# Prompt attention scores of a hybrid decoder step: six 64-row matmuls per key block in place of four 128-row ones

## The chip, the cores and the metric

One core of a Trainium2 chip runs the whole program. The metric is the device time of one execution in microseconds, as the median of several runs. TensorE does the matmuls (PE in the profile, its weight loads PEld), VectorE (DVE), ScalarE (ACT) and GpSimd (POOL) do the elementwise work, SyncE (SP) starts transfers.

## The reference, cut to what matters

The program is one inference step of a two-layer decoder. Layer 0 has, beside a gated MLP, a differential attention with 8 heads. Each head has two components `c` of 64 channels, and the scores of both are taken for every block of 128 queries against all earlier keys; the rest of the step is not touched by the change.

```python
q = rms_norm(zq.reshape(b, l, H_A, 2, DH_A), q_g) * (DH_A ** -0.5)
k = rms_norm(zk.reshape(b, l, H_A, 2, DH_A), k_g)
s = jnp.einsum('bqhcd,bkhcd->bhcqk', q, k)       # + bias, causal
p = jax.nn.softmax(s, axis=-1)
a = p[:, :, 0] - lam * p[:, :, 1]                # o = a @ v
```

The prompt has 1024 tokens (8 blocks of 128); a ninth unit of each head holds 64 sample tokens, whose scores are computed elsewhere.

## The kernel before, in words

The prompt attention is the first stage, lines 261 to 507. It walks over 72 units (head `h`, block `i`), 9 per head, in a software pipeline: at step `s` it emits `otrans` of unit s-12, `av2` of s-8, `av` of s-6, `scores` of s-5, `qk_trans` of s-2 and the projection `qkv_tile` of s, which is 24 matmuls with 384 columns each (three products of high and low halves, lines 143 to 145). The order in which it emits is a priority only. The tile framework simulates the program while it builds it (`schedule_with_timeline_sim`), and at each moment gives an engine the first instruction in that order whose inputs and buffers are free in the simulation; each engine then runs its list in that fixed order. So instructions of one call can be spread out in an engine's list, and another cost of one instruction can change the list.

All matmuls in question take operands in fp32r, in one pass. To keep the accuracy of fp32, each value is split into a high part and a low part (value minus high part).

`qk_trans` (line 361) turns one block of normalised queries and keys (128 tokens by 128 channels: component 0 in channels 0 to 63, component 1 in 64 to 127) with two transposes on TensorE (L364, L365). Then, for each component in turn, on 64 partitions, it makes the high part of q (L89, called from line 380), the low part of q (L381), a copy of both to the other 64 partitions (L87, called from line 382, on ScalarE), the high part of k (L91, from line 383) and the low part of k into the other 64 partitions (L384). So the 128 rows of a stacked operand hold, for one component, high q twice, or low q twice, against high k over low k.

`scores` (line 387) then has for each block of up to 512 keys and each component two matmuls over 128 rows (L399): high q against (high k, low k), and low q against the same. They add up all four products. The result stands in PSUM under the tag `s`, which has two buffers of two banks each. For i below 4, both components share one buffer, one bank each. For i of 4 and more, each component takes a buffer of its own, so a unit takes both. After the matmuls come, per component, the bias (L405) and the maximum (L407, or one L409 for both), and the exponential (L412, ScalarE), whose end frees the buffer.

Keys stand in `kts[h, j]`, four blocks each; queries in `qs`, two buffers. Unit (h, i) has key blocks j = 0 .. i // 4, with widths 512 for a whole one and 128, 256, 384 or 512 for the last one.

Of the kernel before, what the change touches and what calls it, by code (L numbers as in the profile page):

```python
# [11 lines left out]
F32R = mybir.dt.float32r  # L12
I32 = mybir.dt.int32
AF = mybir.ActivationFunctionType
ALU = mybir.AluOpType
# [9 lines left out]
P = 128  # L25
KT = D // P
H = 8
DH = 64
# [9 lines left out]
PRM = {'ktc': 'a', 'ev': 'p', 'ekm': 'p', 'qem': 'd', 'gm': 2, 'wp': (3, 6), 'at': 'a', 'LQ': 2, 'LS': 5, 'LA': 6, 'L2': 8, 'LO': 12, 'on': 'a', 'oT': 'a', 'qk4': 'p', 'kh': 'd', 'vt': 'a', 'qkc': 'a', 'sq': 'p', 'kg': 'p', 'at0': 'a', 'at1': 'a', 'qh': 'd', 'onm': 'd', 'TS': True, 'p0': 2, 'p1': 2, 'qkb': 3, 'qhb': 2, 'ksb': 3, 'lpq': 2, 'qd': 'a', 'vb': 16, 'atb': 2, 'onb': 4}  # L38
# [24 lines left out]
def rows(i):  # L63
    return P if i < NT - 1 else NS
# [7 lines left out]
def hybrid_step(  # L72
# [8 lines left out]
    pe, act, dve, pool = nc.tensor, nc.scalar, nc.vector, nc.gpsimd  # L81
# [3 lines left out]
    def cpy(e, o, i_, scale=None):  # L85
        if e == 'a':
            act.activation(o, i_, AF.Copy, scale=scale) if scale is not None else act.copy(o, i_)  # L87
        elif scale is not None:
            G[e].tensor_scalar_mul(o, i_, scale)  # L89
        else:  # L90
            G[e].tensor_copy(o, i_)  # L91

    def f32(a):
        return a.bitcast(F32)
# [18 lines left out]
    def const(shape, name, dt=F32):  # L113
        return cp.tile(shape, dt, name=name)
# [68 lines left out]
    if True:  # L183
# [77 lines left out]
        with ExitStack() as p1:  # L261
            pa = p1.enter_context(tc.tile_pool(name="pa", bufs=2))
# [4 lines left out]
            qg = const([P, 1], "qg")  # L267
# [50 lines left out]
            kts, vts = {}, {}  # L318
# [42 lines left out]
            def qk_trans(h, i, qk):  # L361
                r = rows(i)
                tp = ps.tile([P, 512], F32, tag="t", name=f"qkt{h}_{i}", bufs=3)
                pe.transpose(tp[:, 0:r], qk[:r, 0:128], ident[:r, :r])  # L364
                pe.transpose(tp[:, 128:128 + r], qk[:r, 128:256], ident[:r, :r])  # L365
                if i == NT - 1:
                    for c in range(2):
                        q8 = slice(c * DH, (c + 1) * DH)
                        act.activation(qbd[q8, h, :, h // 4, c, :], tp[q8, 0:NS].rearrange("p (b q) -> p b q", b=NB),
                                       AF.Copy, scale=qg[q8])  # L370
                    dve.tensor_copy(ksT[:, h, :], tp[:, 128:128 + NS])
                    return None
                qs = pa.tile([P, 2, 2, P], F32R, tag="qs", name=f"qs{h}_{i}", bufs=PRM["qhb"])
                if i % KW == 0:
                    kts[h, i // KW] = pa.tile([P, 2, KW * P], F32R, tag="ks", name=f"ks{h}_{i}", bufs=PRM["ksb"])
                ks = kts[h, i // KW]
                o = i % KW * P
                for c in range(2):
                    own, oth = slice(c * DH, (c + 1) * DH), slice((1 - c) * DH, (2 - c) * DH)
                    cpy(PRM['qh'], qs[own, c, 0], tp[own, 0:128], qg[own])  # L380
                    dve.scalar_tensor_tensor(qs[own, c, 1], tp[own, 0:128], qg[own], f32(qs[own, c, 0]), ALU.mult, ALU.subtract)  # L381
                    cpy(PRM['qd'], qs[oth, c], f32(qs[own, c]))
                    cpy(PRM['kh'], ks[own, c, o:o + P], tp[own, 128:256])
                    dve.tensor_tensor(ks[oth, c, o:o + P], tp[own, 128:256], f32(ks[own, c, o:o + P]), ALU.subtract)  # L384
                return (qs,)

            def scores(h, i, qs):
                n = (i + 1) * P
                if i < 4:
                    st = ps.tile([P, 2, 512], F32, tag="s", name=f"s{h}_{i}")  # L390
                    sc = [st[:, 0, :], st[:, 1, :]]
                else:
                    sc = [ps.tile([P, 1024], F32, tag="s", name=f"s{h}_{i}_{c}") for c in range(2)]
                for j in range(i // KW + 1):
                    k0 = KW * P * j
                    w = min(KW * P, n - k0)
                    for c in range(2):
                        for l in range(2):
                            pe.matmul(sc[c][:, k0:k0 + w], qs[:, c, l], kts[h, j][:, c, :w], start=(l == 0), stop=(l == 1))  # L399
                nm = pa.tile([P, 2], F32, tag="nm", name=f"nm{h}_{i}")  # L400
                ss = pa.tile([P, 2], F32, tag="ss", name=f"ss{h}_{i}")
                pt = []
                lo = max(0, n - 256)
                for c in range(2):
                    dve.tensor_tensor(sc[c][:, lo:n], sc[c][:, lo:n], tb[:, h, 256 - (n - lo):], ALU.add)  # L405
                    if i >= 4:
                        dve.tensor_reduce(nm[:, c:c + 1], sc[c][:, :n], axis=AX.X, op=ALU.max, negate=True)  # L407
                if i < 4:
                    dve.tensor_reduce(nm, st[:, :, :n], axis=AX.X, op=ALU.max, negate=True)  # L409
                for c in range(2):  # L410
                    pc = pa.tile([P, 1024], F32, tag="p0" if c == 0 else "p1", name=f"p{h}_{i}_{c}", bufs=PRM['p0'] if c == 0 else PRM['p1'])
                    act.activation(pc[:, :n], sc[c][:, :n], AF.Exp, bias=nm[:, c:c + 1], accum_out=ss[:, c:c + 1])  # L412
                    pt.append(pc)
                rr = pa.tile([P, 2], F32, tag="rr", name=f"rr{h}_{i}", bufs=4)
                fac = pa.tile([P, 1], F32, tag="fac", name=f"fac{h}_{i}")
                dve.reciprocal(rr, ss)
                dve.scalar_tensor_tensor(fac, ss[:, 0:1], neglam, rr[:, 1:2], ALU.mult, ALU.mult)
                dve.scalar_tensor_tensor(pt[0][:, :n], pt[1][:, :n], fac, pt[0][:, :n], ALU.mult, ALU.add)  # L418
                return pt[0], rr
# [65 lines left out]
            for s in range(len(units) + max(8, PRM['LO'] + 1)):  # L485
                if s == len(units) - 2:
                    load_gate(0)
                stage(s, PRM['LO'], otr)
                stage(s, PRM['L2'], av2)
                stage(s, PRM['LA'], av)  # L490
                stage(s, PRM['LS'], scores)
                stage(s, PRM['LQ'], qk_trans)
                if 0 <= s - 1 < len(units) and units[s - 1][1] == NT - 1:
                    stage(s, 1, qkv_post)
                if 1 <= s <= NT - 4:
                    xprep(s + 3)
                if s == 1:
                    bias_setup(pa, ps, tb)
                if 20 <= s < 20 + H:
                    bias_sample(tb, s - 20)  # L500
                if s < len(units):
                    h, i = units[s]
                    if i == 3 and h + 1 < H:
                        load_head(h + 1)
                    st_[h, i] = qkv_tile(h, i, Ws[h])
                elif s - len(units) < NPRE:
                    gate_a(*du[s - len(units)], gate_tiles)
# [384 lines left out]
    with ExitStack() as p4:  # L892
# [129 lines left out]
        for n, (c0, cw) in enumerate(CH):  # L1022
            tp = psd.tile([P, 512], F32, tag="x", name=f"rbp{n}", bufs=4)
            for q in range(3):
                i = n * 3 + q
# [390 lines left out]
        i = NT - 1  # L1416
# [79 lines left out]
```

## Time and profile before

| | us |
|---|---|
| median of 3 runs | 1801.37 |
| lowest and highest run | 1799.54, 1802.87 |
| span of the profiled execution | 1806.1 |
| PE busy in the span | 1747.1 |
| DVE busy in the span | 1012.4 |
| ACT busy in the span | 755.4 |

The profile is of one execution; its span is 4.7 us above the median of the runs. PE busy counts modelled ends of pipelined matmuls that overlap, so it is no measure of the work in the array; from the start of one matmul to the start of the next is the better one. "PEclk" is the clock that TensorE was granted, in parts of full speed.

### The profile page before, as it was taken

To read this page: it belongs to the slowest core of one execution; us is meant where nothing else is said; L and a number is where in the kernel's file an instruction comes from. 1 tells how busy PE (TensorE), PEld (TensorE's weight loads), DVE (VectorE), ACT (ScalarE), POOL (GpSimd) and SP (SyncE) were. 2 spreads that over 40 slices of the span, in tenths; PEclk is the share of its full clock that TensorE was granted. 3 is DMA by queue.
4 is the path that set the end of the run, shared out by engine and by line. 5 is a ranking of instruction groups with operands and counts; after the bars stand their busy time and mean duration, and the time that the engine had idled before them with its cause. 6 is when DMAs were issued, how large, how long until landed. Compare 5 with 4: busy or idle time off the path is not lost.

```text
span 1806.1 us, 31855 instructions
## 1 busy us (share of the span) xinstructions
PE 1747.1 (97%) x11429; PEld 1629.0 (90%) x11429; DVE 1012.4 (56%) x2223; ACT 755.4 (42%) x1934; POOL 609.3 (34%) x893
## 2 busy tenths in 40 slices
PE   7999999999999899999899999999999999998999
PEld 6798999999999888889899999999999999996777
DVE  5898888988983233223832342444354455667442
ACT  4566656666664222223222232333343334345241
POOL 4555646655653221112721200044111232235230
PEclk8999999999999999999999999999999999999999
DMA  7102202211213766746221262432334244438741
GB/s 211 52 23 73 68 20 67 67 43 43 66 59 104 243 202 232 236 165 213 59 79 54 92 199 74 129 97 82 94 116 152 80 126 123 130 111 260 240 130 71
DMA packets 223302, 211.62 MB, mean 117 GB/s; under 512 B 22286, under 2 KB 201143, under 8 KB 223143
## 3 DMA queue, kind: packets, MB, share of 16 engines
q1 hardware_dynamic: 203510, 194.35, 34.7%
q10 hardware_dynamic: 19632, 15.21, 2.8%
q8 instruction: 91, 1.49, 0.4%
q14 instruction: 69, 0.56, 0.1%
HBM read 151.35 MB, written 56.24 MB: 115 GB/s over the span
## 4 chain that ended last, share of the span: by engine, by line
PE 62%; DVE 16%; DMA 9%; ACT 4%; POOL 4%; issue 4%; SPq 0%; ACTq 0%; POOLq 0%; DVEq 0%
PE o L1373 5%; PE yo L143 3%; PE yo L145 3%; PE yo L144 3%; PE vg L143 3%; PE vg L144 3%; PE vg L145 3%; DMA oT_d<-oTr 2%; DVE p L418 2%; PE zv L143 1%; PE zv L144 1%; PE zv L145 1%; PE o L434 1%; PE s L399 1%; PE qkv L143 1%
## 5 line engine op out<-in xcount | busy, mean ns | idle before, releaser
L412 ACT ACTIVATE p<-s,nm 128x256 f32<-128x256 f32 (+7 forms) x128 | 95.0, 747 | 38.3 <-DVE nm L409 22.3
L399 PE MATMUL s<-ks,qs 128*128 128x512 f32 (+3 forms) x384 | 96.5, 364 | 2.8 <-DVE ks L384 1.4
L87 ACT CAST qs<-qs 64x256 fp32r<-64x256 f32 x128 | 51.7, 404 | 76.8 <-DVE qs L381 74.2
L1120 POOL TENSOR_TENSOR e<-e,k 128x256 f32<-128x256 f32 (+1 forms) x50 | 42.4, 853 | 117.1 <-ACT e L1117 100.8
L338 POOL TENSOR_TENSOR sq<-qk 128x256 f32<-128x256 f32 (+1 forms) x72 | 46.9, 652 | 95.0 <-ACT qk L87 94.2
L434 PE MATMUL o<-v,at 128*128 128x128 f32 x576 | 76.8, 279 | 1.6 <-ACT at L87 1.6
L399 PEld LDWEIGHTS s<-ks,qs 128*128 128x128 f32 x384 | 64.9, 190 | 12.6 <-ACT p L412 2.8
L434 PEld LDWEIGHTS o<-v,at 128*128 128x128 f32 x576 | 71.4, 193 | 4.2 <-ACT at L87 2.6
L131 POOL TENSOR_TENSOR s<-s,mhalf 128x4 f32<-128x4 f32 (+1 forms) x72 | 73.3, 1018 | 5.3
L837 DVE TENSOR_TENSOR yp<-yp,yo 128x384 f32<-128x384 f32 (+1 forms) x48 | 25.3, 530 | 74.5 <-ACT yp L836 41.7
L407 DVE TENSOR_REDUCE nm<-s 128x1 f32<-128x640 f32 (+3 forms) x64 | 65.2, 1019 | 1.2
L747 POOL TENSOR_TENSOR u<-u,th 128x384 f32<-128x384 f32 (+1 forms) x24 | 28.7, 1194 | 99.9 <-DVE th L746 99.4
L405 DVE TENSOR_TENSOR s<-s,tb 128x256 f32<-128x256 f32 (+1 forms) x128 | 52.8, 412 | 8.9 <-PE s L399 5.6
L418 DVE SCALAR_TENSOR_TENSOR p<-p,fac,p 128x128 f32<-128x128 f32 (+3 forms) x64 | 55.1, 861 | 1.7
L1373 PE MATMUL o<-w1h,oh 128*128 128x512 f32 x128 | 53.0, 414 | 2.5 <-ACT oh L1350 2.5
L87 ACT COPY at<-atp 128x512 f32<-128x512 f32 (+2 forms) x96 | 44.5, 481 | 20.0 <-PE atp L427 19.8
L746 DVE SCALAR_TENSOR_TENSOR th<-th,gb 128x384 f32<-128x384 f32 (+1 forms) x24 | 12.6, 524 | 69.0 <-ACT th L745 69.0
L1373 PE MATMUL o<-w1l,oh 128*128 128x512 f32 x128 | 50.8, 397 | 0.0
L1373 PE MATMUL o<-w1h,ol 128*128 128x512 f32 x128 | 50.3, 407 | 0.0
L427 PE MATMUL atp<-cf,p 128*128 128x128 f32 x288 | 46.8, 275 | 1.9 <-DVE p L418 1.8
L343 POOL TENSOR_TENSOR qk<-qk,s 128x256 f32<-128x256 f32 (+1 forms) x72 | 46.6, 647 | 4.7
L381 DVE SCALAR_TENSOR_TENSOR qs<-qkt,qg,qs 64x128 fp32r<-64x128 f32 x128 | 44.5, 348 | 3.6
(825 smaller groups left out, 6340.4 us busy)
## 6 DMA issues: line engine op xcount, KB each, us to landing
kp<-in_cache_k SPq DMA_DIRECT2D x32, 512.0 KB
vp<-in_cache_v SPq DMA_DIRECT2D x32, 512.0 KB
or<-oT_d SPq DMA_DIRECT2D x16, 384.0 KB
vb_d<-zs SPq DMA_DIRECT2D x36, 128.0 KB
oT_d<-ob SPq DMA_DIRECT2D x8, 544.0 KB
gt<-g_d SPq DMA_DIRECT2D x34, 128.0 KB
xt<-in_x_prompt SPq DMA_DIRECT2D x8, 512.0 KB
out<-v ACTq DMA_DIRECT2D x64, 64.0 KB
```

The costliest lines, as they stand in the source:

```text
L87: act.activation(o, i_, AF.Copy, scale=scale) if scale is not None else act.copy(o, i_)
L131: pool.tensor_tensor(dst, dst, mhalf[:dst.shape[0], :n], ALU.pow)
L143: pe.matmul(out, lh, rh, start=(s == 0), stop=False)
L144: pe.matmul(out, lh, rl, start=False, stop=False)
L145: pe.matmul(out, ll, rh, start=False, stop=(s == n - 1))
L399: pe.matmul(sc[c][:, k0:k0 + w], qs[:, c, l], kts[h, j][:, c, :w], start=(l == 0), stop=(l == 1))
L405: dve.tensor_tensor(sc[c][:, lo:n], sc[c][:, lo:n], tb[:, h, 256 - (n - lo):], ALU.add)
L407: dve.tensor_reduce(nm[:, c:c + 1], sc[c][:, :n], axis=AX.X, op=ALU.max, negate=True)
L412: act.activation(pc[:, :n], sc[c][:, :n], AF.Exp, bias=nm[:, c:c + 1], accum_out=ss[:, c:c + 1])
L418: dve.scalar_tensor_tensor(pt[0][:, :n], pt[1][:, :n], fac, pt[0][:, :n], ALU.mult, ALU.add)
L434: pe.matmul(op[:, :P], at[:, j * P:(j + 1) * P], vts[h, j], start=(j == 0), stop=(j == i))
L1373: pe.matmul(it.mp[:r], lh[:, k, :r], rh[k][:, cs], start=(k == 0 and a == 0), stop=(k == KT - 1 and a == 2))
```

## The change

Component 0 stays in partitions 0 to 63 and component 1 in 64 to 127. `qk_trans` makes the high and low parts of q and k over all 128 partitions at once, for both components: four VectorE instructions per unit in place of eight, and no copy on ScalarE. `scores` has three products per key block and component (high by high, high by low, low by high; low by low is dropped), each a matmul over the 64 rows of its component, and runs the two components in turn for each product. The two components of one product use different rows of the array and different PSUM banks.

```diff
-                qs = pa.tile([P, 2, 2, P], F32R, tag="qs", name=f"qs{h}_{i}", bufs=PRM["qhb"])
+                qs = pa.tile([P, 2, P], F32R, tag="qs", name=f"qs{h}_{i}", bufs=PRM["qhb"])
...
-                for c in range(2):
-                    own, oth = slice(c * DH, (c + 1) * DH), slice((1 - c) * DH, (2 - c) * DH)
-                    cpy(PRM['qh'], qs[own, c, 0], tp[own, 0:128], qg[own])
-                    dve.scalar_tensor_tensor(qs[own, c, 1], tp[own, 0:128], qg[own], f32(qs[own, c, 0]), ALU.mult, ALU.subtract)
-                    cpy(PRM['qd'], qs[oth, c], f32(qs[own, c]))
-                    cpy(PRM['kh'], ks[own, c, o:o + P], tp[own, 128:256])
-                    dve.tensor_tensor(ks[oth, c, o:o + P], tp[own, 128:256], f32(ks[own, c, o:o + P]), ALU.subtract)
+                cpy(PRM['qh'], qs[:, 0], tp[:, 0:128], qg)
+                dve.scalar_tensor_tensor(qs[:, 1], tp[:, 0:128], qg, f32(qs[:, 0]), ALU.mult, ALU.subtract)
+                cpy(PRM['kh'], ks[:, 0, o:o + P], tp[:, 128:256])
+                dve.tensor_tensor(ks[:, 1, o:o + P], tp[:, 128:256], f32(ks[:, 0, o:o + P]), ALU.subtract)
...
-                    for c in range(2):
-                        for l in range(2):
-                            pe.matmul(sc[c][:, k0:k0 + w], qs[:, c, l], kts[h, j][:, c, :w], start=(l == 0), stop=(l == 1))
+                    for l, (ql, kl) in enumerate(((0, 0), (0, 1), (1, 0))):
+                        for c in range(2):
+                            cr = slice(c * DH, (c + 1) * DH)
+                            pe.matmul(sc[c][:, k0:k0 + w], qs[cr, ql], kts[h, j][cr, kl, :w], start=(l == 0), stop=(l == 2))
```

## Rows read from the trace of the kernel before

**Rows 1.** The page: busy us, share of the span, instructions of each engine.
```profile
PE 1747.1 (97%) x11429; PEld 1629.0 (90%) x11429; DVE 1012.4 (56%) x2223; ACT 755.4 (42%) x1934; POOL 609.3 (34%) x893
```

**Rows 2.** Busy time by stretch, columns PE, PEld, DVE, ACT, POOL, PEclk, DMA, GB/s.
```profile
45.00:553.00 508.00, 495.30 (x3089) 464.86 (x3088) 447.88 (x1121) 326.26 (x958) 291.35 (x509) 0.99 0.18 54
...
553.00:1806.00 1253.00, 1217.84 (x8174) 1134.61 (x8172) 541.20 (x1063) 409.10 (x934) 297.83 (x349) 0.99 0.45 139
```

**Rows 3.** Waits, 45 to 553 us: who waited for whom, us, times, longest.
```profile
PEld s L399 <- ACT p L412: 2.8, 7, 0.6
...
PEld s L399 <- ACT qs L87: 2.4, 5, 0.5
...
PE s L399 <- DVE ks L384: 1.4, 4, 0.4
```

**Rows 4.** Instructions by form, 45 to 553 us: count | busy us, mean ns | idle before.
```profile
L399 PE MATMUL s<-ks,qs 128*128 128x512 f32 x192 | 62.3, 424 | 1.2 <-ACT p L412 1.0
L87 ACT CAST qs<-qs 64x256 fp32r<-64x256 f32 x128 | 51.7, 404 | 76.8 <-DVE qs L381 74.2
L381 DVE SCALAR_TENSOR_TENSOR qs<-qkt,qg,qs 64x128 fp32r<-64x128 f32 x128 | 44.5, 348 | 3.6
L89 DVE TENSOR_SCALAR qs<-qkt,qg 64x128 fp32r<-64x128 f32 x128 | 44.3, 346 | 3.3 <-PE qkt L365 1.3
L384 DVE TENSOR_TENSOR ks<-qkt,ks 64x128 fp32r<-64x128 f32 x128 | 36.9, 288 | 4.1
L91 DVE CAST ks<-qkt 64x128 fp32r<-64x128 f32 x128 | 36.0, 281 | 0.0
...
L89 DVE TENSOR_SCALAR on<-on,ms 128x128 f32<-128x128 f32 x60 | 23.9, 398 | 6.9 <-POOL ms L131 5.8
```

**Rows 5.** Chain of waits, 100 to 200 us: start, us; L399 with widths 512, 256, 384, 128.
```profile
109.33 1.11 PE o L434 x10
110.45 0.93 PE s L399 x4
...
118.93 0.24 PE s L399 x2
...
126.38 0.35 PE s L399 x2
...
178.67 0.18 PE s L399 x2
```

**Rows 6.** PE in order of time, 399 to 405 us: start, us.
```profile
399.96 0.96 PE L399 MATMUL s<-ks,qs 128*128 128x512 f32 x4 [0.15 <-ACT p L412]
...
403.72 0.94 PE L399 MATMUL s<-ks,qs 128*128 128x512 f32 x4
```

**Rows 7.** ACT in order of time, 399 to 402 us.
```profile
399.03 0.78 ACT L412 ACTIVATE p<-s,nm 128x640 f32<-128x640 f32 x1
...
400.54 0.81 ACT L412 ACTIVATE p<-s,nm 128x640 f32<-128x640 f32 x1
```

**Rows 8.** PE, then PEld, in order of time, 67 to 70 us.
```profile
67.35 0.52 PE L399 MATMUL s<-ks,qs 128*128 128x384 f32 x2
67.81 0.46 PE L309 MATMUL xtp<-cf,xn 64*128 64x64 f32 x4
68.19 0.62 PE L399 MATMUL s<-ks,qs 128*128 128x384 f32 x2
68.75 0.46 PE L309 MATMUL xtp<-cf,xn 64*128 64x64 f32 x4
...
67.81 0.32 PEld L309 LDWEIGHTS xtp<-cf,xn 64*128 64x128 f32 x4 [0.26 <-DVE xl L138]
...
69.13 0.19 PEld L143 LDWEIGHTS qkv<-wq0h,xh 128*128 128x128 f32 x1
69.24 0.19 PEld L144 LDWEIGHTS qkv<-wq0l,xh 128*128 128x128 f32 x1
```

**Rows 9.** PE in order of time, 617 to 621 us: the sample scores' 32-column tiles.
```profile
617.78 1.92 PE L550 MATMUL ssc<-kT,qbd 128*32 128x512 f32 x16
```

## The prediction

> **What bounds the kernel now.** I read the page first, then the busy times by stretch, then the waits of the attention stage, and last TensorE's instructions in order of time. PE is busy for 97% of the span [rows 1], and in the stage that the change touches (45 to 553 us) for 495 of 508 us, at a granted clock of 0.99; DVE is at 448, ACT at 326 [rows 2]. So TensorE's own list of instructions sets the stage, with 12.7 us in which it isn't busy at all. The waits agree: what TensorE waits for from the operands and buffers of the scores are single microseconds in total, 2.8, 2.4 and 1.4 [rows 3]. DVE is close behind, but a faster DVE can give back no more than those 12.7 us, as long as TensorE's list isn't shorter. The 1253 us after the stage have PE at 97% too and none of the changed code [rows 2], so what the stage gains or loses, the end gains or loses.
>
> **Elementwise work.** Per unit, the change takes away four DVE instructions and two ACT copies, and makes four DVE instructions twice as tall. The price of an instruction on 64 partitions is 346 ns (L89), 348 (L381), 281 (L91) and 288 (L384), each 128 times [rows 4]. An L89 of the same 128 columns over 128 partitions took 398 ns [rows 4], on another operand, so I take height as nearly free: 64 units at 1.26 us less, 81 us of DVE (70 if all cost 398), and 51.7 us of ACT. Both engines have idle time beside TensorE, so of that only what TensorE waits for counts: at least 0, at most 12.7 us [rows 2]. I take 8, near the 6.6 us of the three waits on what the change makes shorter [rows 3].
>
> **The score matmuls, if they ran as written.** In the chain of waits, runs without a stall give the time of one matmul from start to start: 0.93 us for four of 512 columns, so 0.23; 0.24 for two of 256, so 0.12; 0.35 for two of 384, 0.175; 0.18 for two of 128, 0.09 [rows 5]. With four products, a head has for i below 4 (one width each) 4 x (0.09 + 0.12 + 0.175 + 0.23) = 2.46 us, and for i from 4 to 7 the same plus four whole blocks, 2.46 + 4 x 0.93 = 6.18 us. Eight heads: 69 us (the counts agree: 192 matmuls of 512 columns [rows 4]). If the two components of a product run side by side, three pairs stand in place of four matmuls, a quarter less: -17.3 us. If they run one after the other, six stand in place of four: +34.6 us. Nothing in this kernel runs 64-row tiles side by side, but 32-column tiles do: 16 records of 512 columns took 1.92 us [rows 9], where ten records of the same type with 128 columns take 1.11, so 0.44 for one of 512 and 7.1 for 16 [rows 5]. That is nearly four at a time, so I take it that two row tiles overlap too. The Trainium skill (TensorE: Matmul & The Clock Gate, Part 3) says the same of row tiles, starts about 4 ns apart, but gives a measured 3.07x for four; an estimate by that share (0.77 of ideal) would leave almost nothing of the gain of a pair. No run here shows it.
>
> **Which of them are side by side.** This decides the sum. For i of 4 and more, each component has its own PSUM buffer, and a unit needs both; a buffer comes free when the exponential of the unit before has read it. Those ends lie apart: the exponentials of i = 4 begin at 399.03 and 400.54 [rows 7], and the scores of i = 5 stand in TensorE's list at 399.96 (the wait is on L412) for component 0 and at 403.72 for component 1, with projections between [rows 6]. In all 32 such units the two components are separate runs, 1 to 7 us apart, as in these rows. In the changed text, high by high of component 0 is followed by that of component 1, whose buffer isn't free yet; the planner passes over it, as it does now, and takes the next two products of component 0. So these units get three products on one half of the array, alone, and later three on the other half: 6.18 becomes 9.27, +3.1 a head, +24.7 us. For i below 4 both components share one buffer. They are apart now too, but there the second component's operands are made after the first's; in the change both come at once, so I take them as pairs: -0.62 a head, -4.9 us. The other end is that two weight loads don't overlap: a load took 0.11 us before the next could start [rows 8], six make 0.66, which for the narrow blocks is more than now (0.36, 0.48) and gives +1.7 us in place of -4.9.
>
> **Going in and out of 64-row tiles.** This trace has 64-row matmuls among 128-row ones. From 67.35 to 68.19 us, two matmuls of 384 columns (0.35) and four 64-row transposes (loads 0.06 apart, 0.24) take 0.84: 0.25 too much. The two matmuls of 384 behind them take 0.56 up to the next transposes, where the first two took 0.46: another 0.10 [rows 8]. So a trip costs 0.35 us, and the first fp32r load inside it isn't hidden either (0.11 against the transposes' 0.06): 0.40. Every run of scores becomes a trip. Units with i of 4 and more have two runs each, 64 in all, the others one, 32: 96 x 0.40 = +38.4 us. Its lower end is 0.20, where a trip begins in a stall that is there anyway, as at 399.96.
>
> **Sum.** +24.7 - 4.9 + 38.4 - 8 = +50 us on the profiled span of 1806.1, so 1856; the median of the runs is 4.7 below the span: 1851. I say 1850. With the lower ends (trips at 0.20, the full 12.7 back) it is 1801.4 + 24.7 - 4.9 + 19.2 - 12.7 = 1828, with the upper ends (nothing back, loads in turn) 1801.4 + 24.7 + 1.7 + 38.4 = 1866. The stage's transposes, projections and transfers are neither more nor fewer; the copy's queue, ACT, is only shorter.
>
> **Rivals.**
> (1) All components are paired, because the planner's list, with half the DVE work and no copy, no longer finds the second buffer late. For it speaks that the list comes from a simulation that I don't see, and that the planner gives the paired products the better place in the order once both buffers are free; against it, that a buffer's release hangs on L412 and the maximum before it, which don't change. Then there are 64 trips: -17.3 + 25.6 - 12.7 (TensorE's list hardly grows, so DVE's relief reaches it in full) = -4.4, 1797. It decides below (17.3 + 12.7) / 0.40 = 75 trips: with fewer the kernel is faster. I give it 18 in 100, just over half of that on the faster side.
> (2) No pair overlaps, or all components are split, for i below 4 too: 34.6 + 128 x 0.40 - 8 = +78, 1879. For it, that nearly all of them are split now; against it, the shared buffer. 12 in 100.
> (3) The trips are mostly hidden (0.10 each) with the same split: 24.7 - 4.9 + 9.6 - 8 = +21, 1823. Against it stands [rows 8], where nothing hid them. 8 in 100.
> (4) In a run on one half of the array each weight load waits for the matmul before it: 64 runs of three or six matmuls, 384 in all, 0.11 us each, +42 on my sum, 1893. The Trainium skill (the same page, Part 3, what overlaps) would have it so, loads overlapping only where the row group differs. The trace speaks against it: the four 64-row transposes, all on the same rows, have loads 0.06 apart that take 0.14 each [rows 8]. 2 in 100.
> That the change doesn't do what it says is no rival of its own: rival 2 holds it.
>
> **How the numbers follow.** My forecast has 60 in 100, the rivals 18, 12, 8 and 2. Of the forecast and rivals 2 to 4 all is slower, 82 in 100. Rival 1 gives 10 to faster by over 0.2% and 8 to within 0.2%, which is about 3.6 us and about what a measurement of this kernel can tell from no change. The range from 1800 to 1880 holds the forecast with its ends (1828 to 1866), rivals 2 and 3, and the upper half of rival 1; left out are the lower half of rival 1, rival 4 and a tail of the second.
>
> **What would show it.** In the changed profile, TensorE's list for i of 4 and more has runs of one component, six matmuls in a row at 0.23 or less from start to start, and component 1 some us later; for i below 4, L399's successor has pairs that start within hundredths of a microsecond. About 0.4 us more than the matmuls' own time lies around each run, as in [rows 8]. DVE's busy time in the stage falls by about 80 us and ACT's by 52, and the stage ends about 50 us later. I am wrong if the runs hold both components for i of 4 and more, if the trips cost much less than 0.4, or if TensorE waits for something else by then.

## The result and the profile after

The change makes the kernel slower: 1825.35 us against 1800.53 (medians of four runs each), a ratio of 1.0128, 95% interval 1.0106 to 1.015. So it costs 23 us by the ratio (19 to 27) and 25 by the medians, half of the 50 that were forecast, and on the forecast's side of no change. The profiled execution after has a span of 1827.4 us, before 1806.1: 21.3 more.

The page of the changed kernel, engines and the costliest group of the scores (in this kernel the score matmuls stand on L397):

```profile
PE 1784.9 (98%) x11621; PEld 1640.0 (90%) x11621; DVE 924.6 (51%) x1967; ACT 700.6 (38%) x1806; POOL 615.8 (34%) x893
...
L397 PE MATMUL s<-ks,qs 64*128 64x512 f32 (+3 forms) x576 | 107.0, 369 | 0.0
```

The busy times of the attention stage, same columns as [rows 2]:

```profile
45.00:553.00 508.00, 507.45 (x3143) 453.64 (x3142) 343.45 (x837) 257.77 (x795) 285.90 (x495) 1.00 0.17 50
```

The elementwise part did what was forecast: in the same 508 us DVE has 343 us of work where it had 448, ACT 258 where it had 326 (not all of the stage: it ends later now). PE is busy for 507.45 of 508 us; the 12.7 us in which it was not are gone. The elementwise instructions by form, 45 to 575 us, answer to [rows 4]:

```profile
L379 DVE SCALAR_TENSOR_TENSOR qs<-qkt,qg,qs 128x128 fp32r<-128x128 f32 x64 | 22.1, 345 | 0.9
...
L89 DVE TENSOR_SCALAR qs<-qkt,qg 128x128 fp32r<-128x128 f32 x64 | 22.0, 344 | 14.7 <-PE qkt L365 13.7 <-PE s L397 0.4
...
L381 DVE TENSOR_TENSOR ks<-qkt,ks 128x128 fp32r<-128x128 f32 x64 | 18.1, 283 | 0.5
...
L91 DVE CAST ks<-qkt 128x128 fp32r<-128x128 f32 x64 | 17.8, 279 | 0.0
```

128 partitions cost what 64 did (344 ns against 346 for L89), with half as many instructions: about 80 us of DVE gone, and the copies with them.

Now TensorE in order of time, where head 2 turns to i = 4 (projections left out), and then i = 7 of the same head:

```profile
203.99 1.02 PE L397 MATMUL s<-ks,qs 64*128 64x512 f32 x4
204.93 0.33 PE L364 MATMUL qkt<-cf,qk 128*128 128x128 f32 x1
205.10 0.27 PE L365 MATMUL qkt<-cf,qk 128*128 128x128 f32 x1
205.30 0.43 PE L397 MATMUL s<-ks,qs 64*128 64x128 f32 x2
205.66 0.44 PE L143 MATMUL qkv<-wq2h,xh 128*128 128x384 f32 x1
205.94 0.34 PE L144 MATMUL qkv<-wq2l,xh 128*128 128x384 f32 x1
...
210.04 0.39 PE L432 MATMUL o<-v,at 128*128 128x128 f32 x2
210.36 1.24 PE L397 MATMUL s<-ks,qs 64*128 64x512 f32 x6
211.53 0.55 PE L425 MATMUL atp<-cf,p 128*128 128x128 f32 x3
```

```profile
233.26 1.65 PE L397 MATMUL s<-ks,qs 64*128 64x512 f32 x12
234.84 0.44 PE L143 MATMUL qkv<-wq3h,xh 128*128 128x384 f32 x1
235.12 0.34 PE L144 MATMUL qkv<-wq3l,xh 128*128 128x384 f32 x1
```

In the first, one component's six matmuls (three of 512 columns, three of 128) stand at 203.99 and 205.30, and the other's six at 210.36: apart by 6 us, as forecast, and alone on their half of the array. Besides, two transposes got between the first six, so they make two trips. In the second, all twelve matmuls of i = 7 stand in one run, and it takes 1.58 us up to the next start. Twelve one after the other would take 12 x 0.23 = 2.76. Less about 0.19 for the run's first weight load and for getting out, it is 0.23 for each pair: two row tiles do run side by side, at the price of one. (The two of a pair start 1 to 10 ns apart in this run.) The trip can be read here too: 0.44 stands for a projection of 384 columns that is 0.34 otherwise, and 0.28 lies between its start and the next, where it is 0.17.

I then took the stage apart for every kernel in the same way: from the first score matmul to the last transposed output (54.8 to 579.1 us before, 54.7 to 601.0 after), less the time that each matmul has when nothing disturbs it. These are 0.174 us for 384 columns, 0.148 for 320, 0.11 for one fp32 record of 128, and for scores 0.23, 0.175, 0.12 and 0.09 by width, a pair that starts together (less than 15 ns apart) counted once. What is left is trips and waits; trips are counted in TensorE's list (from a 128-row to a 64-row matmul, all lines) and taken at 0.37 us, of which 0.09 is ahead of the run, 0.10 its first load, 0.09 behind it, and 0.06 to 0.11 the first load of what follows. The last column is a rest, good to a few us. Read gap by gap instead, with no fixed price, the gaps at 64-row matmuls and right behind them have 44 us beyond the undisturbed times after (0.34 a trip), and all other gaps have 3 us after and about 30 before. The profile's own list of waits agrees in kind: what it names for PE and its loads from 45 to 560 us, without what it puts down to "issue", adds up to 39 us before and 10 after.

| kernel | stage | scores' own time | trips | trips x 0.37 | waits (rest) |
|---|---|---|---|---|---|
| before | 524.3 | 68.5 | 11 | 4 | 32 |
| after | 546.3 | 78.4 | 127 | 47 | 1 |
| difference | +22.0 | +9.9 | +116 | +43 | -31 |

All other matmuls are 420 us in both. Behind the stage nothing changed: 1227.0 us are left before, 1226.4 after.

So the result is +10 for the matmuls, +43 for the trips and -31 for waits that are gone, where the forecast had +20, +38 and -8. The question for the experiments was what took the waits away: the lighter elementwise work, or TensorE's longer list, behind which waits disappear. A third possibility goes with both: the planner builds each kernel's list anew, and another order can have other waits.

### The profile page after: what moved, and what is told of

The parts are those of the page before. It is cut to its first block, busy times and chain, and to the rows that moved or that the text cites. A ratio compares the mean times of both kernels' runs of the same rounds, so it can differ in the third digit from the quotient of the medians.

```text
span 1827.4 us, 31816 instructions
## 1 busy us (share of the span) xinstructions
PE 1784.9 (98%) x11621; PEld 1640.0 (90%) x11621; DVE 924.6 (51%) x1967; ACT 700.6 (38%) x1806; POOL 615.8 (34%) x893
## 4 chain that ended last, share of the span: by engine, by line
PE 82%; DMA 7%; DVE 4%; issue 2%; POOL 2%; ACT 2%; SPq 0%; ACTq 0%; POOLq 0%; DVEq 0%
PE s L397 5%; PE qkv L143 5%; PE o L1371 5%; PE qkv L144 5%; PE qkv L145 5%; PE o L432 4%; PE yo L143 3%; PE yo L145 3%; PE yo L144 3%; PE vg L143 3%; PE vg L144 3%; PE vg L145 3%; PE atp L425 2%; PE zv L143 2%; PE zv L144 2%
## 5 line engine op out<-in xcount | busy, mean ns | idle before, releaser
L397 PE MATMUL s<-ks,qs 64*128 64x512 f32 (+3 forms) x576 | 107.0, 369 | 0.0
L397 PEld LDWEIGHTS s<-ks,qs 64*128 64x128 f32 x576 | 70.4, 184 | 24.5 <-issue 10.8
L87 ACT COPY qk<-qkv 128x256 f32<-128x256 f32 x64 | 23.7, 370 | 150.9 <-issue 116.4
L340 DVE TENSOR_REDUCE s<-sq 128x4 f32<-128x256 f32 (+1 forms) x72 | 29.9, 415 | 75.5 <-POOL sq L338 75.4
```

Source lines behind the costliest of these rows:

```text
L397: pe.matmul(sc[c][:, k0:k0 + w], qs[cr, ql], kts[h, j][cr, kl, :w], start=(l == 0), stop=(l == 2))
```

## The experiments

Each kernel's expectations were written before it ran; ratios are to the kernel before, run on the same chip.

**The elementwise part alone.** Scores in `e1_prep_alone`, with the change's `qk_trans`:

```diff
-                    for l, (ql, kl) in enumerate(((0, 0), (0, 1), (1, 0))):
-                        for c in range(2):
-                            cr = slice(c * DH, (c + 1) * DH)
-                            pe.matmul(sc[c][:, k0:k0 + w], qs[cr, ql], kts[h, j][cr, kl, :w], start=(l == 0), stop=(l == 2))
+                    for c in range(2):
+                        for l in range(2):
+                            pe.matmul(sc[c][:, k0:k0 + w], qs[:, l], kts[h, j][:, c, :w], start=(l == 0), stop=(l == 1))
```

> The elementwise part of the change alone: four VectorE instructions over 128 partitions and no copies, with the four 128-row matmuls of before on these operands (so the scores mix both components; the output is not the reference's). No 64-row tiles, the same matmul time as before. Theory: the lighter elementwise work gives TensorE back about 27 us, so 1774. Rival, as the forecast had it: it gives back about 8, so 1792.

1790.7 us, ratio 0.9966 (0.9948 to 0.9984). That is 6 to 8 us faster (3 to 9 by the interval), the forecast's 8, and not the 27 of the theory that I had formed from the trace of after. With TensorE's list nearly as long as before (17 trips in place of 11), waits fall from 32 to 21 us, and new ones show up, which the waits from 45 to 560 us name:

```profile
PEld o L431 <- ACT at L87: 10.8, 14, 2.4
...
PE o L431 <- ACT at L87: 6.4, 11, 2.0
```

TensorE now waits for the transposed weights `at` that ACT copies, a wait of 2.6 us in the kernel before (the loads' part):

```profile
PEld o L434 <- ACT at L87: 2.6, 5, 0.5
```

So the lighter work alone doesn't explain the 31 us.

**Six matmuls over all 128 rows.** No 64-row tiles, no pairs: the longest list that the scores can have.

```diff
-                            cr = slice(c * DH, (c + 1) * DH)
-                            pe.matmul(sc[c][:, k0:k0 + w], qs[cr, ql], kts[h, j][cr, kl, :w], start=(l == 0), stop=(l == 2))
+                            pe.matmul(sc[c][:, k0:k0 + w], qs[:, ql], kts[h, j][:, kl, :w], start=(l == 0), stop=(l == 2))
```

> The changed kernel with its six matmuls per key block over all 128 rows instead of 64 (the scores mix both components; the output is not the reference's): no trips into 64-row tiles and no overlap of the two components. Theory: +34.6 us for six matmuls in place of four and -27 for the lighter elementwise work, 1808, so faster than the change. Rival: the trips are cheap and the elementwise work gave little, then this is 1800.5 + 34.6 - 8 = 1827, no faster than the change.

1812.5 us, ratio 1.0076 (1.0053 to 1.0098): between the theory's 1808 and the rival's 1827, nearer to the theory (though the 27 in it isn't what the elementwise part gives alone), and faster than the change, although nothing runs side by side in it. Against the run before, the list is longer by 34 us and the time by 21.8; waits fall from 21 to 7. Over a third of the added work isn't in the time: as much of the waits is gone.

**The removed load put back.** The change with four DVE instructions on 64 partitions and two copies per unit that nobody reads:

```diff
+                dm = pa.tile([P, 2, P], F32R, tag="dm", name=f"dm{h}_{i}", bufs=1)
+                lo_, hi_ = slice(0, DH), slice(DH, 2 * DH)
+                cpy(PRM['qh'], dm[hi_, 0], tp[hi_, 0:128], qg[hi_])
+                dve.scalar_tensor_tensor(dm[hi_, 1], tp[hi_, 0:128], qg[hi_], f32(dm[hi_, 0]), ALU.mult, ALU.subtract)
+                cpy(PRM['qd'], dm[lo_], f32(qs[hi_]))
+                cpy(PRM['kh'], dm[hi_, 0], tp[hi_, 128:256])
+                dve.tensor_tensor(dm[hi_, 1], tp[hi_, 128:256], f32(dm[hi_, 0]), ALU.subtract)
+                cpy(PRM['qd'], dm[hi_], f32(qs[lo_]))
```

> The changed kernel with the removed elementwise load put back beside the new one: four VectorE instructions on 64 partitions and two ScalarE copies per unit into a buffer that nobody reads. If the gain of the change's elementwise part came from the load of VectorE and ScalarE, nearly all of it goes: 1825 + 20 to 27 = about 1850. Rival: it came from the shorter chain ahead of the second component's scores, not from the load, then 1825 to 1832.

1843.0 us, ratio 1.0246 (1.0224 to 1.0267), 18 to 21 more than the change. It looks like the load's price, but the parts say something else: waits rise by only 7 us (1 to 8); the other 9 come from the planner's list, which now has 93 pairs where the change has 139 (scores 87 us in place of 78). The load matters, but as waits only for 7 of the 16 us by which the stage is longer; the first run had 11 us of waits from it.

**The components in turn.** The two inner loops swapped:

```diff
-                    for l, (ql, kl) in enumerate(((0, 0), (0, 1), (1, 0))):
-                        for c in range(2):
-                            cr = slice(c * DH, (c + 1) * DH)
+                    for c in range(2):
+                        cr = slice(c * DH, (c + 1) * DH)
+                        for l, (ql, kl) in enumerate(((0, 0), (0, 1), (1, 0))):
```

> The changed kernel with the three products of component 0 ahead of the three of component 1, so nothing is side by side but the last and the first. Theory: six matmuls in place of four, +34.6 us, about 120 trips of 0.36, +43, and -27 for the elementwise work: about 1852, so 27 slower than the change, which is what pairing gives. Rival: pairing gives nothing because both tiles share a port, then it is about 1825 as the change.

1828.0 us, ratio 1.0166 (1.0143 to 1.0188), 3 to 7 above the change, which the two intervals don't tell apart. It looks like the rival, but the run didn't make what it was meant to: the planner still put 113 pairs side by side (122 if starts up to 20 ns apart are counted; the change has 139 either way), with the same 127 trips. The 17 to 26 pairs fewer cost 2 to 4 us of the scores' own time. What pairing gives was not settled by this run; the run of i = 7 above shows it.

**The price of a trip, twice.** On the kernel before, and on the one with six full-row matmuls, one more matmul of 128 columns stands ahead of each unit's scores, once over 64 rows and once, as a control, over 128. On the kernel before, over 64 rows (the control has `0:P` in place of `0:DH`):

```diff
+                    if j == 0:
+                        pe.matmul(sc[0][:, :P], qs[0:DH, 0, 0], kts[h, 0][0:DH, 0, :P], start=True, stop=True)
```

> The kernel before with one more matmul of 128 columns ahead of each unit's scores, over 64 rows (its result is overwritten): 64 trips into 64-row tiles and nothing else of the change. Theory: a trip costs about 0.38 us beside the matmul's own 0.09, so 64 x 0.47 = +30, 1830. Rival: trips cost 0.20 or are hidden in stalls, 1800.5 + 64 x 0.29 = 1819 or less.

> The control of the run before: the same extra matmul over all 128 rows, so without a trip. Both theories: 64 x 0.09 = +6, 1806; the difference of the two runs is the price of 64 trips (24 us by the theory, 13 or less by the rival).

1816.3 us (1.0101, 1.0067 to 1.0134) and 1809.6 (1.0055, 1.0031 to 1.0079): the difference is 7 us for 64 trips, good to about 7 by the intervals, the rival's side. Taken alone, that would be a trip at 0.1 us. But with the trips at the same 0.37, the waits fall from 30 to 15 us, and the profile's own list of waits says so too: what it names for PE and its loads from 45 to 560 us adds up to 37 us in the control and to 22 with the trips (PE and loads counted each, "issue" left out). The longest in the control is this one, of which the run with the trips has 0.7 us left, on the loads alone:

```profile
PEld o L436 <- DVE ks L384: 4.7, 6, 1.9
...
PE o L436 <- DVE ks L384: 3.7, 6, 1.6
```

With the trips:

```profile
PEld o L436 <- DVE ks L384: 0.7, 4, 0.2
```

The same on the kernel with six full-row matmuls, which has few waits:

> The kernel with six full-row matmuls (scores mix both components; the output is not the reference's) and one more 64-row matmul of 128 columns ahead of each unit's scores (overwritten). The stage has only about 7 us of stalls there, so the price of 64 trips can't vanish in them: against the next run 64 x 0.37 = 24 us more, at least 17. Rival (a trip really costs a tenth of a microsecond, as the two runs on the kernel before suggest by their times): 7 more.

> The control of the run before: the same extra matmul over 128 rows, no trip: 1812 + 64 x 0.09 = 1818.

1838.9 us and 1818.6: 20.4 us for 64 trips, good to about 8, so 0.32 each, with waits from 8 to 5. In this pair TensorE's two built lists are the same, 3470 records in the same order by operands and width, so nothing but the trips differs. The price of a trip holds where TensorE has little to wait for, and half to two thirds of it vanish in the kernel before (7 us by the times, 9 by the stages in the table below). But the lists of that first pair are not the same: matched in order, 2738 of their 3276 records agree. So 15 us of waits went with 64 trips and a rebuilt list together; how much of it the trips alone covered isn't shown. With the same list it was 3 of 8.

**A third query buffer.** The kernel before with `'qhb': 3` and, for the room, `'vb': 14`:

> The kernel before with three buffers for the split queries in place of two (and 14 for the values in place of 16, to make room). If TensorE's idle time before came from the second component's operands being late because a query buffer came free late, this gives back part of it: 1785 to 1795. If it came from the load of VectorE and ScalarE, no change: 1800.

1799.4 us, ratio 1.001 (0.9994 to 1.0026): no change, 31 us of waits left. The waits of before don't hang on that buffer alone.

**All pairs, fewer trips.** If pairs and trips set the change's time, a kernel that pairs everything should win. Here one PSUM buffer holds both components of a key block:

```diff
-                    sc = [ps.tile([P, 1024], F32, tag="s", name=f"s{h}_{i}_{c}") for c in range(2)]
...
+                sts = [ps.tile([P, 2, 512], F32, tag="s", name=f"s{h}_{i}_{j}") for j in range(nj)]
...
+                            pe.matmul(sts[j][:, c, :ws[j]], qs[cr, ql], kts[h, j][cr, kl, :ws[j]], start=(l == 0), stop=(l == 2))
```

> The changed kernel with the PSUM buffers cut the other way: for i of 4 and more, one buffer per key block that holds both components, instead of one per component (maxima and exponentials by key block, joined by a minimum and a sum). Both components of every product then find their buffer free at once, so all 288 pairs are side by side (matmul time 51 us in place of 78 in the change's trace) and a unit has one trip, 70 to 90 in place of 127 (26 to 33 us in place of 47). TensorE's list: 420 + 51 + 30 = 501 us in the stage, plus stalls of 5 to 20, against 546 in the change and 524 before. Theory: 1784 to 1804, so at least 20 faster than the change and about as fast as before or faster. Rival: the time of the change doesn't hang on pairs and trips, or the four more ScalarE and VectorE steps per unit take the gain back: 1815 to 1830.

1839.2 us, ratio 1.0223 (1.0194 to 1.0252): slower than the change. Its list came out as meant, 266 pairs, scores at 55 us, 98 trips; with 420 + 55 + 36 that is 511 us, less than before with all its waits. But the waits are 51 us. TensorE in order of time, i = 5 and then i = 6 of head 2, and what it waits for (45 to 560 us; scores on L393):

```profile
217.53 1.32 PE L393 MATMUL s<-ks,qs 64*128 64x512 f32 x12
...
226.51 0.33 PE L432 MATMUL atp<-cf,p 128*128 128x128 f32 x1 [0.38 <-ACT osq L444]
...
227.85 0.96 PE L393 MATMUL s<-ks,qs 64*128 64x512 f32 x6 [1.01 <-ACT p L416]
```

```profile
PEld s L393 <- ACT p L416: 17.5, 37, 1.3
...
PE s L393 <- ACT p L416: 8.3, 10, 1.1
```

A buffer now comes free only when both components' exponentials have read it. In the change, the split into components, which cost it its pairs, let the next unit's first scores start while the second component was still in its exponential. But these two lines are 26 us of the 75.5 that the list of waits names for PE and its loads (without "issue"). The kernel also has 192 exponentials in place of 128, 153 us of ScalarE in place of 121 (their accumulator reads included), and this run doesn't part that rival from the buffer: which of them made most of the 51 us is open.

The stage of all kernels, as in the table above:

| kernel | stage | scores' own time | trips | waits (rest) |
|---|---|---|---|---|
| prep alone | 516.1 | 68.5 | 17 | 21 |
| six full rows | 536.1 | 102.8 | 17 | 7 |
| six full rows, no trip | 542.8 | 108.4 | 16 | 8 |
| six full rows and trip | 563.3 | 108.4 | 80 | 5 |
| before, same 128 rows | 529.5 | 74.1 | 15 | 30 |
| before and trip | 538.6 | 74.1 | 79 | 15 |
| prep load back | 562.4 | 87.3 | 128 | 8 |
| components in turn | 549.4 | 82.5 | 127 | 0 |
| three query buffers | 523.6 | 68.5 | 11 | 31 |
| slots by key block | 562.5 | 55.3 | 98 | 51 |

## Why the prediction was right or wrong

**What bounds the kernel: right, but read too far.** TensorE's list sets the stage. The step that failed is the term for waits, -8 and at most -12.7: about -31 was measured. That PE isn't busy for 12.7 us was taken as all that could be given back. It isn't: busy time counts modelled ends, a matmul of 384 columns as 0.33 to 0.35 us where the next starts after 0.17, so a wait of up to 0.17 behind each doesn't show. From start to start, 32 us of the stage were waits, and 31 of them are gone. The text ahead of the prediction says that the starts are the better measure, but the bound was still taken from busy time.

**Elementwise work: right by itself.** The forecast's 8 us is what the part gives alone (6 to 8 measured, waits -11). Height is free here, and about 80 us of DVE and 52 of ACT went. (The 70 us given for the case that all cost 398 ns should be 60; it enters no sum.)

**The sum: its terms don't add.** The forecast put work on TensorE's list at full price and took waits off only for the lighter DVE. But waits also fell when the list got longer: by 15 us with 64 trips and the old elementwise work, which cost 7, and by 14 with 34 us of matmuls and the new one. The lighter work alone took 11. In the change both bear on the same 32 us. How they share them can't be said from these runs, since the planner makes another list each time, and part of the fall may be that list; that waits fell with each of them is shown. Of the 28 us between the forecast's +50 and the stage's +22, 23 are the waits and 10 the pairs, and the trips were 5 more than forecast.

**Which products are side by side: half right.** At i = 4 and i = 6 the components are apart, as forecast, in the seven heads after the first. At i = 7 in six of these heads, and partly at i = 5, they are in one run: rival 1, for part of the units. That is 139 pairs (9 of them of unequal widths) of 288 where the forecast had 96 (the units below 4), and +9.9 us where it had +19.8. The reason given, that the second buffer is always late, is too coarse. ScalarE in order of time, the second exponentials of i = 4 and of i = 6 of head 2:

```profile
214.93 0.79 ACT L410 ACTIVATE p<-s,nm 128x640 f32<-128x640 f32 x1
...
229.56 1.01 ACT L410 ACTIVATE p<-s,nm 128x896 f32<-128x896 f32 x1 [1.04 <-DVE nm L405]
```

The first ends at 215.7, where the scores of i = 5 start at 215.61, and the second component joins after a few matmuls. The other ends at 230.6, 2.7 us ahead of the scores of i = 7 at 233.26, so both buffers are free by then. What the planner found in its simulation isn't on record; this is what the trace shows.

**Pairs below i = 4: right in size, wrong in the count of runs.** They are pairs, but for two products at i = 2 of each head after the first, and the narrow ones overlap too: inside a run, one pair of 128 columns follows the other after 0.11 us (so at 116.46, and in the kernel with slots by key block), so two loads run side by side, which refutes the forecast's upper end. But transposes of the softmax weights stand in the middle of many of these runs:

```profile
240.91 0.33 PE L397 MATMUL s<-ks,qs 64*128 64x128 f32 x2
241.16 0.66 PE L425 MATMUL atp<-cf,p 128*128 128x128 f32 x4
241.75 0.44 PE L397 MATMUL s<-ks,qs 64*128 64x128 f32 x4
242.12 0.44 PE L143 MATMUL qkv<-wq3h,xh 128*128 128x384 f32 x1
```

So there are 117 runs of scores in place of 96 and 116 trips more than before, +43 us in place of +38.

**The price of a trip: right.** 0.40 forecast from four transposes; 0.34 to 0.37 in the trace of after, 0.32 in time where hardly a wait hides it.

**Rivals.** Rival 1 came true for the units named, not as a whole. Rival 3's time (1823) is the nearest to the result, but not by its mechanism: the trips are not cheap, they stand at full price in TensorE's list, and what made up for them was waits that went elsewhere in the stage. Rival 4 is refuted: six matmuls on one half of the array, at 210.36, take 1.17 us to the next start, of which three of 512 columns alone are 0.69 and three of 128 about 0.28, and 0.19 the trip's ends. The loads are hidden behind matmuls on the same rows. The rule of the Trainium skill that this rival came from (TensorE: Matmul & The Clock Gate, Part 3, loads overlap only where the row group differs) doesn't hold in this trace; its other statement there, that tiles on different rows run at once, does, and at full value for two.

## What to carry to other kernels

On an engine that sets the pace, work and waits need not add up: ask how much of its time is waits from start to start, not by busy time, before putting an added instruction at full price or a saved one at full gain. A 64-row tile among 128-row work pays a trip of a third of a microsecond each time, so it pays only in long, paired runs: here a pair of 512 columns saves a quarter of four matmuls, 0.23 us per key block, less than one trip. And when a list comes from a planner, count what stands side by side in the built list; an experiment that changes the text may not change the list in the way meant, and only a run and a control with the same list differ in nothing but the thing tested.

## What the runs showed of the hardware that was not expected

Two matmuls on the two row halves, into different PSUM banks, cost what one does, down to 128 columns (0.11 us a pair, 0.23 at 512). Loads for both halves overlap (a load alone took 0.11 us before the next could start [rows 8], and so did a pair of 128 columns with both of its loads), and loads for the same half are hidden behind its own matmuls (six of one component at 210.36: 0.23 us from start to start at 512 columns). What costs is the change between 64 and 128 rows: about 0.09 us in, 0.09 out, and one weight load that isn't hidden on either side (0.10 and 0.06 to 0.11).
